# State-space blocks with rows by token, built by two vector passes and four shifted scalar-engine copies

## The chip, the cores and the metric

The kernel runs on one core of one Trainium2 chip. The core has a matrix engine (PE in the profile, TensorE), a vector engine (DVE), a scalar engine (ACT), a general engine (POOL, GpSimd) and a queue that issues the transfers (SP). Each takes its own instructions in order and waits for the others by semaphores. The metric is the time of one execution on the device in microseconds. The kernel before took 2307.09 us (median of three runs, 2300.07 to 2309.19).

## The reference, cut to what matters

The program is two transformer-like blocks on 1024 tokens of width 1024. The change lies in the state-space branch of the first block. It has 32 groups of 16 channels, each with 64 complex states:

```python
def s5_branch(u, ...):
    ug = uf.reshape(bsz, seqlen, 32, 16)
    x_re, x_im = k * (B @ ug)             # complex, 64 states a group
    # h[t] = a * h[t-1] + x[t], complex, by an associative scan over the tokens
    y = einsum('gcp,lbgp->blgc', c_re, h_re) - einsum('gcp,lbgp->blgc', c_im, h_im)
    y = y + d_skip * uf
    y = gelu(y)
    y = y * sigmoid(y @ w_glu + b_glu)
```

The rest (layer norm, latent attention, output projections; a second block with dilated and neighbourhood attention and a gated convolution) is not touched.

## The kernel before, in words

Nothing is written here in the order in which it runs. The program is written by layers, and a scheduler with a timeline of its own then sets the order of every engine's instructions (`schedule_with_timeline_sim=True` where the program is built). So a change of a few instructions also moves others.

In the first block, `block1` projects the normalised tokens with `w_in`. Each of 15 column tiles is two accumulations of 24 matmuls of 512 columns (three products of split operands for each of eight input tiles, lines 135 to 137). The weights of a tile are loaded into `wst`, then ACT rounds them to `wh` (line 102) and POOL computes the rest `wl` (line 111). The first four column tiles are the input u of the state-space branch, which ACT copies out and SP stores to `u_d` with the 8 tokens of a block side by side. Between the later column tiles stand eight calls of `ssm_unit`, one for four groups each. So PE has the dense tiles to do while the units run through the other engines.

A unit treats 8 tokens as one block, so 1024 tokens are 128 blocks. For each of its four groups it needs a 128 x 128 matrix TM from 8 x 16 inputs of a block to its 8 x 16 outputs (block-lower-triangular, and the same along each diagonal), a matrix EM from inputs to states and CS from states to outputs:

- ES (DVE and POOL) is transposed by PE to `sps` and copied by ACT to EM (line 653 and after); KR and CS give `kps`, the effect of an input on an output 0 to 7 tokens later (line 658). DVE adds the skip term `dd` to lag 0.
- DVE builds TM from `kps` in eight passes. Row p of TM is an input (channel c, token s of the block, p = 8c + s), and its columns have to be shifted by s. So pass s multiplies `kps` by a column of the table `cst` that is one where p % 8 = s and adds it s tokens further on: one tensor_scalar of 512 elements and seven scalar_tensor_tensor (lines 90 and 86) of 448, 384, ..., 64 elements, each on all 128 partitions.
- Rotations R (DVE and POOL), the decay RH (POOL, with a zero at the start of each group), the products px = EM U (line 690), the rotated inputs xr, a scan on DVE (line 700), rotation back to h.
- py = TM U + CS h (lines 711 and 712), gelu on ACT, and the store of y by SP.

U is read from `u_d` by one transfer a unit. EM, CS, TM, R and U have two buffers, the others one.

Of the kernel before, what the change touches and what calls it, by code (L numbers as in the profile page):

```python
# [10 lines left out]
F32 = mybir.dt.float32  # L11
F32R = mybir.dt.float32r
I32 = mybir.dt.int32
ALU = mybir.AluOpType
AF = mybir.ActivationFunctionType
# [21 lines left out]

CST = {}
_o = 0
for _n, _w in (("inv_freq", 1), ("sgn", 1), ("shift", 8), ("chan", 16)):  # L40
    CST[_n] = (_o, _w)
    _o += _w
NCST = _o
# [4 lines left out]
def ap_of(t, offset, dims):  # L48
    return bass.AP(tensor=t.tensor, offset=t.offset + offset, ap=dims)


class Kernel:
# [394 lines left out]
    def ssm_open(self):  # L447
        self.sp2, self.spps = self.open("ssmb"), self.open("ssmps", space=PSUM)

    def exp_small(self, x, n, pool, name):  # L450

        nc = self.nc
        a = pool.tile([128, n], F32, name=name + "a")
        r = pool.tile([128, n], F32, name=name + "r")
        p = pool.tile([128, n], F32, name=name + "p")
        e = pool.tile([128, n], I32, name=name + "e")
        self.ts(r, x, -150.0, 89.0, ALU.max, ALU.min)
        M = 12582912.0
        self.ts(a, r, 1.0 / math.log(2.0), M, ALU.mult, ALU.add)
        self.ts(a, a, M, None, ALU.subtract)  # L460
        hi = 0.693359375
        lo = math.log(2.0) - hi
        self.stt(r, a, -hi, r, ALU.mult, ALU.add)
        self.stt(r, a, -lo, r, ALU.mult, ALU.add)
        c = [1.0 / math.factorial(i) for i in range(8)]
        self.ts(p, r, c[7], None, ALU.mult)
        for i in range(6, 0, -1):
            self.stt(p, p, c[i], r, ALU.add, ALU.mult)
        self.ts(p, p, 1.0, None, ALU.add)
        self.ts(a, a, -127.0, 128.0, ALU.max, ALU.min)  # L470
        self.ts(e, a, 127.0, 8388608.0, ALU.add, ALU.mult)
        self.tt(p, p, e.bitcast(F32), ALU.mult)
        return p
# [35 lines left out]
    def ssm_tables(self):  # L509
        nc, I, keep = self.nc, self.I, self.sp  # L510
        p = self.st_
        T = lambda name, shape, dt=F32: p.tile(shape, dt, name=name)
        K = lambda name, shape, dt=F32: keep.tile(shape, dt, name=name)
# [5 lines left out]
        nc.sync.dma_start(self.Cs, I["ssm_bc"][:, 2])  # L519
        self.C2 = K("C2", [128, 32, 16])  # L520
        nc.sync.dma_start(self.C2, I["ssm_bc"][:, 3])
        self.dsk = K("dsk", [128, 32])
        nc.sync.dma_start(self.dsk, I["ssm_d"])
        pos = T("pos", [128, 256], I32)
        for q in range(4):
            nc.sync.dma_start(pos[32 * q:32 * q + 32, :],
# [1 line left out]
        sgn = self.cst[:, CST["sgn"][0]:CST["sgn"][0] + 1]  # L528
# [22 lines left out]
        w = K("pw", [128, 2, 9, 32])  # L551
# [6 lines left out]
        for m in (1, 2, 4):  # L558
            br = wr[:, m:m + 1, :].to_broadcast([128, m, 32])
            bi = wi[:, m:m + 1, :].to_broadcast([128, m, 32])  # L560
            a, b = slice(1, m + 1), slice(m + 1, 2 * m + 1)
# [62 lines left out]
    def ssm_unit(self, u):  # L624

        nc, p, pp = self.nc, self.sp2, self.spps
        b, q = divmod(u, 2)
        G = slice(4 * u, 4 * u + 4)
        T = lambda name, shape, bufs=1, tag=None: p.tile(shape, F32, name=name, tag=tag or name, bufs=bufs)
        f = lambda t: t.rearrange("p a b -> p (a b)")  # L630

        U = T("U", [128, 4, 128], 2)
        nc.sync.dma_start(U, ap_of(self.u_d[b], 64 * q * 1024, [[128, 128], [16 * 1024, 4], [1, 128]]))

        ES = T("ES", [128, 4, 16, 8])
        CS = T("CS", [128, 4, 16, 8], 2)
        tm = T("tm", [128, 4, 16, 8])
        for out, pw, a, c, op in ((ES, self.pv, self.kB1, self.kB2, ALU.add),
                                  (CS, self.pw, self.Cs, self.C2, ALU.subtract)):

            o, t = (y.rearrange("p g c e -> p g e c") for y in (out, tm))
            sh = [128, 4, 8, 16]
            w = lambda i: pw[:, i, 0:8, G].rearrange("p e g -> p g e")[:, :, :, None].to_broadcast(sh)
            x = lambda y: y[:, G][:, :, None, :].to_broadcast(sh)
            self.tt(o, x(a), w(0), ALU.mult, eng=nc.gpsimd)
            self.tt(t, x(c), w(1), ALU.mult)
            self.tt(out, out, tm, op)
        KR = T("KR", [128, 4, 16, 8])
        self.act(KR, self.kB1[:, G][:, :, :, None].to_broadcast([128, 4, 16, 8]), AF.Copy)
        EM = T("EM", [128, 4, 128], 2)  # L650
        ps = pp.tile([128, 4, 128], F32, name="sps", tag="sa", bufs=2)
        for g in range(4):
            nc.tensor.transpose(ps[:, g, :], f(ES[:, g]), self.ident)
        self.act(EM, ps, AF.Copy)

        ps = pp.tile([128, 4, 16, 8], F32, name="kps", tag="sa", bufs=2)
        for g in range(4):
            nc.tensor.matmul(ps[:, g], f(KR[:, g]), f(CS[:, g]), start=True, stop=True)
        o = CST["chan"][0]
        dd = T("dd", [128, 4, 16])  # L660
        self.tt(dd, self.dsk[:, G][:, :, None].to_broadcast([128, 4, 16]),
                self.cst[:, None, o:o + 16].to_broadcast([128, 4, 16]), ALU.mult)
        self.tt(ps[:, :, :, 0], ps[:, :, :, 0], dd, ALU.add)
        TM = T("TM", [128, 4, 16, 8], 2)
        o = CST["shift"][0]
        self.ts(TM, ps, self.cst[:, o:o + 1], None, ALU.mult)
        for s in range(1, 8):
            self.stt(TM[:, :, :, s:], ps[:, :, :, :8 - s], self.cst[:, o + s:o + s + 1], TM[:, :, :, s:], ALU.mult,
                     ALU.add)

        R = T("R", [128, 2, 4, 128], 2)
        rc, rs = R[:, 0], R[:, 1]
        sh = [128, 4, 8, 16]
        v = lambda t: t.rearrange("p g (a b) -> p g a b", a=8)
        A = lambda i: self.RA[:, i, G][:, :, :, None].to_broadcast(sh)
        B = lambda i: self.RB[:, i, G][:, :, None, :].to_broadcast(sh)
        t1 = T("rt", [128, 4, 128])
        self.tt(v(rc), A(0), B(0), ALU.mult, eng=nc.gpsimd)
        self.tt(v(t1), A(1), B(1), ALU.mult)
        self.tt(rc, rc, t1, ALU.subtract)  # L680
        t1 = T("rt", [128, 4, 128])
        self.tt(v(rs), A(1), B(0), ALU.mult, eng=nc.gpsimd)
        self.tt(v(t1), A(0), B(1), ALU.mult)
        self.tt(rs, rs, t1, ALU.add)
        RH = T("RH", [128, 4, 128])
        self.ts(RH, self.rho[:, G][:, :, None].to_broadcast([128, 4, 128]), 1.0, None, ALU.mult, eng=nc.gpsimd)
        nc.gpsimd.memset(RH[:, :, 0:1], 0.0)
        px = pp.tile([128, 4, 128], F32, name="px", tag="sx", bufs=1)
        for g in range(4):
            nc.tensor.matmul(px[:, g, :], EM[:, g, :], U[:, g, :], start=True, stop=True)  # L690
        x2 = T("x2", [128, 4, 128])
        self.act(x2[0:64], px[64:128], AF.Copy)
        self.act(x2[64:128], px[0:64], AF.Copy)
        xr = T("xr", [128, 4, 128])

        self.tt(xr, px, rc, ALU.mult)
        self.tt(x2, x2, rs, ALU.mult)
        self.tt(xr, xr, x2, ALU.subtract)
        gg = T("gg", [128, 4, 128])
        nc.vector.tensor_tensor_scan(f(gg), f(RH), f(xr), 0.0, op0=ALU.mult, op1=ALU.add)  # L700
        g2 = T("g2", [128, 4, 128], 1, "x2")
        self.act(g2[0:64], gg[64:128], AF.Copy)
        self.act(g2[64:128], gg[0:64], AF.Copy)
        h = T("h", [128, 4, 128])
        nc.vector.memset(h[:, :, 0:1], 0.0)
        self.tt(gg, gg, rc, ALU.mult)
        self.tt(g2, g2, rs, ALU.mult)
        self.tt(h[:, :, 1:], gg[:, :, :127], g2[:, :, :127], ALU.add)
        py = pp.tile([128, 4, 128], F32, name="py", tag="sy", bufs=1)
        for g in range(4):  # L710
            nc.tensor.matmul(py[:, g, :], f(TM[:, g]), U[:, g, :], start=True, stop=False)
            nc.tensor.matmul(py[:, g, :], f(CS[:, g]), h[:, g, :], start=False, stop=True)
        y = T("y", [128, 4, 128], 2)
        self.act(y, py, AF.Gelu_apprx_tanh)
        nc.sync.dma_start(ap_of(self.y_d[b], 64 * q * 1024, [[128, 128], [16 * 1024, 4], [1, 128]]), y)
# [1322 lines left out]
def _constants():  # L2038
# [16 lines left out]
    inv = (np.float32(1.0) / np.power(10000.0, e).astype(np.float32)).astype(np.float32)  # L2055
    cst[:, CST["inv_freq"][0]] = np.tile(inv, 4)
    cst[:, CST["sgn"][0]] = np.where(k < 64, -1.0, 1.0)
    o, w = CST["shift"]
    cst[:, o:o + w] = k[:, None] % 8 == np.arange(8)[None]
    o, w = CST["chan"]  # L2060
    cst[:, o:o + w] = k[:, None] // 8 == np.arange(16)[None]

    oh = np.zeros((34, L1W + L2W), np.float32)
    d1 = np.arange(L1W) - 191
# [21 lines left out]
def _layout(v):  # L2086
# [15 lines left out]
    br, bi = f["b_re"][0].transpose(1, 0, 2), f["b_im"][0].transpose(1, 0, 2)  # L2102
    cr, ci = f["c_re"][0].transpose(2, 0, 1), f["c_im"][0].transpose(2, 0, 1)
    r["ssm_bc"] = A(np.stack([np.concatenate(t) for t in ((br, bi), (bi, br), (cr, ci), (ci, cr))], 1))
    r["ssm_d"] = A(np.repeat(f["d_skip"][0].reshape(32, 16).T, 8, axis=0))
    r["w_glu"] = A(_tiles(f["w_glu"][0]))
    wq = f["w_uq"][0].reshape(256, 4, 192)
    wq = np.concatenate([wq[:, :, :128].reshape(256, 512), wq[:, :, 128:160].reshape(256, 128),
# [53 lines left out]
```

## Time and profile before

| | |
|---|---|
| median of three runs | 2307.09 us |
| the profiled execution's own time | 2299.86 us |
| its span | 2298.1 us |
| PE busy over the span | 2116.0 us (92%) |
| DVE busy | 1574.8 us (69%) |
| ACT busy | 983.3 us (43%) |
| POOL busy | 1157.1 us (50%) |
| first instruction of a unit's TM to the last | 121.1 to 308.1 us |

The profile page gives each engine's busy time as a share of the span, then the span in forty slices. The queries on the trace cut out a stretch: which engine is busy for how long in it, which instruction waits for which, and each instruction in order of time. A share over the whole span says nothing of a stage: the units run between about 100 and 320 us, and only their rows tell what limits that stage. A PE that is listed busy counts pipelined matmuls, so what it does not do is seen in its idle time and in the clock that it was granted.

### The profile page before, as it was taken

Reading aid. Unit: us, or ns where it says so; the run is one execution under the profiler, and the core shown is the slowest. Engines: PE = TensorE matmul, PEld = TensorE weight load, DVE = VectorE, ACT = ScalarE, POOL = GpSimd, SP = SyncE. Lnnn points to the kernel's source line nnn. Section 1 sums busy time; section 2 is a strip of 40 time slices with the busy share of each in tenths; the row PEclk is TensorE's granted clock in tenths of the full one; section 3 lists DMA queues with packets and bytes.
Section 4 is the critical chain, followed back from the end, with each engine's and each line's share of the span. In section 5 each row is a group of like instructions: output and inputs, shape, how many; then the busy total and the mean of one; then the engine's idle time right before and its main releaser. Section 6 shows DMA issues by size and latency. Waiting matters only on the chain. (4 is left out here: it accounts for less than half of the span.)

```text
span 2298.1 us, 29156 instructions
## 1 busy us (share of the span) xinstructions
PE 2116.0 (92%) x10144; PEld 1753.3 (76%) x10144; DVE 1574.8 (69%) x2610; ACT 983.3 (43%) x1737; POOL 1157.1 (50%) x742
## 2 busy tenths in 40 slices
PE   6998898899989989999999898995999999999888
PEld 4786777777867778888878786884778888877667
DVE  8969966651587155545766744438877777788997
ACT  4323345432256267656444433224444444454333
POOL 4625547655455455565313425326555555534464
PEclk8998999999999999999999999998999999999998
DMA  7433335555554645655345635441222222232233
GB/s 275 136 93 115 97 121 179 177 160 197 191 179 157 203 128 179 184 167 163 99 142 163 195 116 192 155 137 51 75 90 83 83 83 83 83 137 89 85 115 115
DMA packets 187264, 314.32 MB, mean 137 GB/s; under 512 B 43544, under 2 KB 85100, under 8 KB 187116
## 3 DMA queue, kind: packets, MB, share of 16 engines
q1 hardware_dynamic: 187116, 312.45, 42.3%
q8 instruction: 80, 1.31, 0.2%
q14 instruction: 68, 0.56, 0.1%
HBM read 226.70 MB, written 80.96 MB: 134 GB/s over the span
## 5 line engine op out<-in xcount | busy, mean ns | idle before, releaser
L111 POOL TENSOR_TENSOR wl<-wst,wh 128x1024 fp32r<-128x1024 f32 (+2 forms) x159 | 393.9, 2479 | 500.9 <-ACT wh L102 446.8
L102 ACT ACTIVATE wh<-wst 128x1024 fp32r<-128x1024 f32 (+1 forms) x164 | 168.2, 1028 | 241.5 <-PE ps L136 110.4
L83 POOL TENSOR_TENSOR acc<-acc,wa 128x512 f32<-128x512 f32 x84 | 109.9, 1309 | 14.5 <-ACT wa L102 11.0
L135 PE MATMUL ps<-xh,wh 128*128 128x512 f32 x256 | 103.9, 406 | 4.8 <-DVE kb L83 2.7
L135 PE MATMUL ps<-h0h,wh 128*128 128x512 f32 x256 | 104.3, 407 | 0.7 <-ACT wh L102 0.7
L135 PE MATMUL ps<-h1h,wh 128*128 128x512 f32 x256 | 101.1, 395 | 3.3 <-DVE qz L86 2.1
L137 PE MATMUL ps<-h0h,wl 128*128 128x512 f32 x256 | 103.5, 404 | 0.3 <-POOL wl L111 0.2
L136 PE MATMUL ps<-h0l,wh 128*128 128x512 f32 x256 | 103.3, 403 | 0.0
L136 PE MATMUL ps<-xl,wh 128*128 128x512 f32 x256 | 102.3, 400 | 0.0
L137 PE MATMUL ps<-xh,wl 128*128 128x512 f32 x256 | 102.3, 399 | 0.0
L136 PE MATMUL ps<-h1l,wh 128*128 128x512 f32 x256 | 101.3, 396 | 0.0
L83 POOL TENSOR_TENSOR tb<-rt,grid 128x384 f32<-128x384 f32 x48 | 42.9, 901 | 115.5 <-DVE mx L886 87.8
L137 PE MATMUL ps<-h1h,wl 128*128 128x512 f32 x256 | 100.9, 394 | 0.0
L111 POOL TENSOR_TENSOR wl<-z,wh 128x1024 fp32r<-128x1024 f32 (+1 forms) x38 | 85.8, 2258 | 27.0 <-ACT wh L102 19.9
L1902 PE MATMUL pd<-Ah,wh 128*128 128x512 f32 x224 | 87.2, 403 | 9.5 <-DVE s L83 5.6
L1902 PE MATMUL pd<-Al,wh 128*128 128x512 f32 x224 | 89.1, 399 | 4.4 <-DVE Al L111 4.4
L83 DVE TENSOR_TENSOR z<-r,wst 128x512 f32<-128x512 f32 x40 | 69.4, 1736 | 24.3 <-POOL wl L111 23.5
L1902 PE MATMUL pd<-Ah,wl 128*128 128x512 f32 x224 | 84.1, 395 | 0.8 <-POOL wl L111 0.8
L90 POOL TENSOR_SCALAR wa<-wa,sc 128x512 f32<-128x512 f32 x36 | 57.8, 1605 | 50.4 <-DMA wa<-in_w_ada 43.2
L886 DVE CUSTOM_DVE_ANT_0 sp<-sp,tab 128x256 f32<-128x256 f32 (+1 forms) x128 | 52.8, 424 | 39.1 <-PE sp L163 22.6
L102 ACT ACTIVATE a<-a 128x1024 f32<-128x1024 f32 x22 | 23.4, 1062 | 108.8 <-DVE a L86 108.8
L102 ACT ACTIVATE P<-sp,st 128x256 f32<-128x256 f32 (+1 forms) x128 | 58.9, 463 | 24.2 <-DVE st L886 23.0
(591 smaller groups left out, 7176.5 us busy)
## 6 DMA issues: line engine op xcount, KB each, us to landing
wa<-in_w_ada SPq DMA_DIRECT2D x96, 256.0 KB, 3.5
wst<-in_w_in SPq DMA_DIRECT2D x47, 512.0 KB, 3.8
wst<-in_w_up SPq DMA_DIRECT2D x26, 512.0 KB, 3.3
a_d<-a SPq DMA_DIRECT2D x22, 512.0 KB, 2.6
wst<-in_w_down SPq DMA_DIRECT2D x22, 512.0 KB, 3.6
as<-a_d SPq DMA_DIRECT2D x22, 512.0 KB, 3.5
r<-in_w_up SPq DMA_DIRECT2D x20, 512.0 KB, 3.2
wst<-in_w_out SPq DMA_DIRECT2D x16, 512.0 KB, 3.3
```

What stands on the lines that cost most here:

```text
L83: (eng or self.nc.vector).tensor_tensor(out, a, b, op)
L90: (eng or self.nc.vector).tensor_scalar(out, a, s1, None, op0=op0)
L102: self.nc.scalar.activation(out, a, f, **kw)
L111: self.last_lo = e.tensor_tensor(lo, y, hi.bitcast(F32), ALU.subtract)
L135: first = mm(ps, wh, xh, start=start, stop=False)
L136: mm(ps, wh, xl, start=False, stop=False)
L137: mm(ps, wl, xh, start=False, stop=stop)
L886: self.nc.vector.tensor_tensor_reduce(out=s, in0=s, in1=tab, scale=-1.0, scalar=-NEG, op0=ALU.add, op1=ALU.min, accum_out=m)
L1902: nc.tensor.matmul(ps, w[u][:, 128 * k:128 * k + 128], x[v], start=start and k == i == 0, stop=k == 1 and i == 2, skip_group_check=True)
```

## The change

- The rows of TM are put in the order p = 16s + c (token first). U is loaded to match, by four transfers a unit in place of one. ES and KR get the same order of columns, so both are now written in the order in which they lie. The tables `cst` and `ssm_d` follow.
- TM is now built in three steps. Two DVE passes, over the rows of even and of odd tokens, make Z, which is `kps` unshifted or shifted by one token. Then four copies by ACT, one for each 32 partitions (two tokens), put Z into TM shifted by 0, 2, 4 and 6 tokens. TM has two fixed buffers that POOL zeroes once; the part left of the shift is never written again.
- The skip term `dd` is computed once for all groups in `ssm_tables`, not in each unit.
- The decay RH is spread along the tokens by ACT, not by POOL. POOL still writes the zero.

```diff
-for _n, _w in (("inv_freq", 1), ("sgn", 1), ("shift", 8), ("chan", 16)):
+for _n, _w in (("inv_freq", 1), ("sgn", 1), ("even", 1), ("odd", 1), ("chan", 16)):
...
+        self.TM = [self.sp2.tile([128, 4, 16, 8], F32, name=f"TM{i}") for i in range(2)]
+        for x in self.TM:
+            self.nc.gpsimd.memset(x, 0.0)
...
+        self.dd = K("dd", [128, 32, 16])
+        self.tt(self.dd, dsk[:, :, None].to_broadcast([128, 32, 16]),
+                self.cst[:, None, o:o + 16].to_broadcast([128, 32, 16]), ALU.mult)
...
         U = T("U", [128, 4, 128], 2)
-        nc.sync.dma_start(U, ap_of(self.u_d[b], 64 * q * 1024, [[128, 128], [16 * 1024, 4], [1, 128]]))
-
-        ES = T("ES", [128, 4, 16, 8])
+        for g in range(4):
+            nc.sync.dma_start(U[:, g], ap_of(self.u_d[b], (64 * q + 16 * g) * 1024, [[128, 8], [1024, 16], [1, 128]]))
+
+        ES = T("ES", [128, 4, 8, 16])
...
-            o, t = (y.rearrange("p g c e -> p g e c") for y in (out, tm))
+            tm = T("tm", list(out.shape))
+            o, t = (y if out is ES else y.rearrange("p g c e -> p g e c") for y in (out, tm))
...
-        KR = T("KR", [128, 4, 16, 8])
-        self.act(KR, self.kB1[:, G][:, :, :, None].to_broadcast([128, 4, 16, 8]), AF.Copy)
+        KR = T("KR", [128, 4, 8, 16])
+        self.act(KR, self.kB1[:, G][:, :, None, :].to_broadcast([128, 4, 8, 16]), AF.Copy)
...
-        dd = T("dd", [128, 4, 16])
-        self.tt(dd, self.dsk[:, G][:, :, None].to_broadcast([128, 4, 16]),
-                self.cst[:, None, o:o + 16].to_broadcast([128, 4, 16]), ALU.mult)
-        self.tt(ps[:, :, :, 0], ps[:, :, :, 0], dd, ALU.add)
-        TM = T("TM", [128, 4, 16, 8], 2)
-        o = CST["shift"][0]
-        self.ts(TM, ps, self.cst[:, o:o + 1], None, ALU.mult)
-        for s in range(1, 8):
-            self.stt(TM[:, :, :, s:], ps[:, :, :, :8 - s], self.cst[:, o + s:o + s + 1], TM[:, :, :, s:], ALU.mult,
-                     ALU.add)
+        self.tt(ps[:, :, :, 0], ps[:, :, :, 0], self.dd[:, G], ALU.add)
+
+        Z = T("Z", [128, 4, 16, 8])
+        m = [self.cst[:, CST[n][0]:CST[n][0] + 1] for n in ("even", "odd")]
+        self.ts(Z, ps, m[0], None, ALU.mult)
+        self.stt(Z[:, :, :, 1:], ps[:, :, :, :7], m[1], Z[:, :, :, 1:], ALU.mult, ALU.add)
+        TM = self.TM[u % 2]
+        for k in range(4):
+            r = slice(32 * k, 32 * k + 32)
+            self.act(TM[r, :, :, 2 * k:], Z[r, :, :, :8 - 2 * k], AF.Copy)
...
-        self.ts(RH, self.rho[:, G][:, :, None].to_broadcast([128, 4, 128]), 1.0, None, ALU.mult, eng=nc.gpsimd)
+        self.act(RH, self.rho[:, G][:, :, None].to_broadcast([128, 4, 128]), AF.Copy)
```

How the order moves is shown at two places; the lines of the kernel after stand some ten further down. The first is DVE from the skip term of the seventh unit on (`kps<-kps,dd`; the rows between belong partly to the unit before it, such as h, and to the gates, gt). Before:

```order
L83 TENSOR_TENSOR kps<-kps,dd 128x64
L83 TENSOR_TENSOR h<-gg,g_2243 128x4x127
L90 TENSOR_SCALAR TM<-kps,cst 128x512
L83 TENSOR_TENSOR dd<-dsk,cst 128x64
L86 SCALAR_TENSOR_TENSOR TM<-kps,cst,TM 128x64x7
L83 TENSOR_TENSOR R<-R,rt 128x512
L86 SCALAR_TENSOR_TENSOR TM<-kps,cst,TM 128x64x6
L83 TENSOR_TENSOR xr<-px,R 128x512
L83 TENSOR_TENSOR x_2381<-x_2381,R 128x512
L83 TENSOR_TENSOR rt<-RA,RB 128x512
L86 SCALAR_TENSOR_TENSOR TM<-kps,cst,TM 128x64x5
```

DVE from the same instruction on, after the change:

```order
L83 TENSOR_TENSOR kps<-kps,dd 128x64
L86 SCALAR_TENSOR_TENSOR gt<-gt,ps 128x512
L83 TENSOR_TENSOR rt<-RA,RB 128x512
L90 TENSOR_SCALAR Z<-kps,cst 128x512
L83 TENSOR_TENSOR ES<-ES,tm 128x512
L83 TENSOR_TENSOR R<-R,rt 128x512
L86 SCALAR_TENSOR_TENSOR Z<-kps,cst,Z 128x64x7
L83 TENSOR_TENSOR tm<-C_607,pw 128x4x8x16
L714 MEMSET h 128x4
L83 TENSOR_TENSOR CS<-CS,tm 128x512
L83 TENSOR_TENSOR xr<-px,R 128x512
L83 TENSOR_TENSOR x_2387<-x_2387,R 128x512
```

Before, the passes over TM run on between the products of the input (xr, x) and beyond them; after, both passes over Z stand ahead of these, and four rows of work lie between the second of them and the product that reads x.

The second place is ACT in the same unit, from the gates' row ahead of its EM on. Before:

```order
L102 ACTIVATE gt<-ps 128x512
L102 ACTIVATE EM<-sps 128x512
L102 ACTIVATE g_2243<-gg 64x512 x2
L102 ACTIVATE KR<-kB_814 128x512
L102 ACTIVATE x_2381<-px 64x512 x2
```

ACT after the change:

```order
L102 ACTIVATE gt<-ps 128x512
L102 ACTIVATE EM<-sps 128x512
L102 ACTIVATE KR<-kB_816 128x512
L102 ACTIVATE TM_1105<-Z 32x512
L102 ACTIVATE TM_1105<-Z 32x64x6
L102 ACTIVATE TM_1105<-Z 32x64x4
L102 ACTIVATE TM_1105<-Z 32x64x2
L102 ACTIVATE y<-py 128x512
L102 ACTIVATE x_2387<-px 64x512 x2
L102 ACTIVATE gt<-ps 128x512
L102 ACTIVATE g_2396<-gg 64x512 x2
L102 ACTIVATE RH<-rho 128x512
```

The four copies into TM, and the gelu of the unit before (y), stand ahead of the two copies of px that give x, and RH follows the two copies g of the scan's result.

## Rows read from the trace of the kernel before

**Rows 1.** The page: span, and busy time and share of each engine.

```profile
span 2298.1 us, 29156 instructions
...
PE 2116.0 (92%) x10144; PEld 1753.3 (76%) x10144; DVE 1574.8 (69%) x2610; ACT 983.3 (43%) x1737; POOL 1157.1 (50%) x742
```

**Rows 2.** Busy time by stretch: length, PE, PEld, DVE, ACT, POOL, clock, DMA, GB/s.

```profile
120.00:160.00 40.00, 40.00 (x214) 33.92 (x214) 21.55 (x37) 12.60 (x22) 11.48 (x10) 1.00 0.44 128
160.00:300.00 140.00, 121.91 (x613) 101.82 (x612) 135.15 (x185) 44.21 (x69) 68.68 (x45) 0.94 0.33 95
180.00:200.00 20.00, 13.44 (x54) 10.97 (x55) 19.91 (x25) 5.02 (x7) 10.63 (x6) 0.74 0.34 106
...
300.00:320.00 20.00, 20.00 (x102) 17.03 (x102) 10.43 (x19) 4.53 (x8) 2.78 (x1) 0.99 0.28 87
```

**Rows 3.** What PE waited for from 160 to 300 us: us, times, longest.

```profile
PE py L712 <- DVE h L83: 5.9, 4, 2.0
PE px L690 <- DVE xr L83: 3.7, 1, 3.7
...
PE py L711 <- DVE TM L86: 2.3, 1, 2.3
```

**Rows 4.** DVE by operation, 160 to 300 us: count, busy us, mean ns, idle before.

```profile
L86 DVE SCALAR_TENSOR_TENSOR TM<-kps,cst,TM 128x448 f32<-128x448 f32 (+6 forms) x42 | 20.1, 484 | 0.2
L83 DVE TENSOR_TENSOR h<-gg,g 128x508 f32<-128x508 f32 x6 | 11.1, 1857 | 0.0
...
L83 DVE TENSOR_TENSOR tm<-C,pw 128x512 f32<-128x512 f32 x6 | 7.6, 1265 | 0.0
L83 DVE TENSOR_TENSOR tm<-kB,pv 128x512 f32<-128x512 f32 x5 | 6.6, 1317 | 0.0
...
L83 DVE TENSOR_TENSOR dd<-dsk,cst 128x64 f32<-128x64 f32 x6 | 2.1, 358 | 0.0
```

**Rows 5.** DVE in order of time, 261 to 294 us: start, us, instruction.

```profile
261.10 0.21 DVE L83 TENSOR_TENSOR kps<-kps,dd 128x64 f32<-128x64 f32 x1
...
281.37 0.22 DVE L83 TENSOR_TENSOR kps<-kps,dd 128x64 f32<-128x64 f32 x1
...
283.09 0.67 DVE L86 SCALAR_TENSOR_TENSOR TM<-kps,cst,TM 128x448 f32<-128x448 f32 x1
283.69 0.96 DVE L83 TENSOR_TENSOR R<-R,rt 128x512 f32<-128x512 f32 x1
...
292.18 0.69 DVE L83 TENSOR_TENSOR gg<-gg,R 128x512 f32<-128x512 f32 x1
...
293.64 2.59 DVE L83 TENSOR_TENSOR h<-gg,g 128x508 f32<-128x508 f32 x1
```

**Rows 6.** POOL in order of time, 281 to 294 us.

```profile
281.52 2.58 POOL L83 TENSOR_TENSOR R<-RA,RB 128x512 f32<-128x512 f32 x2 [1.19 <-DVE g L83]
...
290.94 1.77 POOL L90 TENSOR_SCALAR RH<-rho 128x512 f32<-128x512 f32 x1 [5.23 <-DVE gg L700]
...
293.31 2.38 POOL L111 TENSOR_TENSOR wl<-wst,wh 128x1024 fp32r<-128x1024 f32 x1 [0.43 <-ACT wh L102]
```

**Rows 7.** POOL by operation, 160 to 300 us.

```profile
L90 POOL TENSOR_SCALAR RH<-rho 128x512 f32<-128x512 f32 x6 | 9.8, 1636 | 33.8 <-DVE gg L700 33.8
```

**Rows 8.** ACT by shape, 100 to 320 us.

```profile
L102 ACT ACTIVATE x<-px 64x512 f32<-64x512 f32 x16 | 9.5, 593 | 28.7 <-PE px L690 12.2 <-DVE h L83 11.3 <-issue 4.9
...
L102 ACT ACTIVATE wh<-wst 128x256 fp32r<-128x256 f32 x2 | 0.8, 417 | 4.7 <-issue 4.7
...
L102 ACT ACTIVATE li<-lps 8x383 f32<-8x383 f32 x1 | 0.5, 463 | 0.0
```

**Rows 9.** SP's issue of transfers in order of time, 105 to 290 us.

```profile
111.03 0.29 SPq L953 DMA_DIRECT2D oh<-in_oh  x1
...
283.87 0.37 SPq L633 DMA_DIRECT2D U<-u_d  x1
```

**Rows 10.** PE in order of time, 109 to 116 us.

```profile
114.91 1.01 PE L955 MATMUL lps<-oh,rel 34*8 34x511 f32 x2 [2.54 <-DMA oh<-in_oh]
```

More of the change, by code (lines that the diff above doesn't have):

```diff
@@ L521, in ssm_tables @@
         nc.sync.dma_start(self.C2, I["ssm_bc"][:, 3])
-        self.dsk = K("dsk", [128, 32])
-        nc.sync.dma_start(self.dsk, I["ssm_d"])
+        dsk = T("dsk", [128, 32])
+        nc.sync.dma_start(dsk, I["ssm_d"])
+        o = CST["chan"][0]
+        self.dd = K("dd", [128, 32, 16])
+        self.tt(self.dd, dsk[:, :, None].to_broadcast([128, 32, 16]),
+                self.cst[:, None, o:o + 16].to_broadcast([128, 32, 16]), ALU.mult)
         pos = T("pos", [128, 256], I32)
@@ L632, in ssm_unit @@
         U = T("U", [128, 4, 128], 2)
-        nc.sync.dma_start(U, ap_of(self.u_d[b], 64 * q * 1024, [[128, 128], [16 * 1024, 4], [1, 128]]))
-        ES = T("ES", [128, 4, 16, 8])
+        for g in range(4):
+            nc.sync.dma_start(U[:, g], ap_of(self.u_d[b], (64 * q + 16 * g) * 1024, [[128, 8], [1024, 16], [1, 128]]))
+        ES = T("ES", [128, 4, 8, 16])
         CS = T("CS", [128, 4, 16, 8], 2)
-        tm = T("tm", [128, 4, 16, 8])
         for out, pw, a, c, op in ((ES, self.pv, self.kB1, self.kB2, ALU.add),
                                   (CS, self.pw, self.Cs, self.C2, ALU.subtract)):
-            o, t = (y.rearrange("p g c e -> p g e c") for y in (out, tm))
+            tm = T("tm", list(out.shape))
+            o, t = (y if out is ES else y.rearrange("p g c e -> p g e c") for y in (out, tm))
             sh = [128, 4, 8, 16]
@@ L658, in ssm_unit @@
             nc.tensor.matmul(ps[:, g], f(KR[:, g]), f(CS[:, g]), start=True, stop=True)
-        o = CST["chan"][0]
-        dd = T("dd", [128, 4, 16])
-        self.tt(dd, self.dsk[:, G][:, :, None].to_broadcast([128, 4, 16]),
-                self.cst[:, None, o:o + 16].to_broadcast([128, 4, 16]), ALU.mult)
-        self.tt(ps[:, :, :, 0], ps[:, :, :, 0], dd, ALU.add)
-        TM = T("TM", [128, 4, 16, 8], 2)
-        o = CST["shift"][0]
-        self.ts(TM, ps, self.cst[:, o:o + 1], None, ALU.mult)
-        for s in range(1, 8):
-            self.stt(TM[:, :, :, s:], ps[:, :, :, :8 - s], self.cst[:, o + s:o + s + 1], TM[:, :, :, s:], ALU.mult,
-                     ALU.add)
+        self.tt(ps[:, :, :, 0], ps[:, :, :, 0], self.dd[:, G], ALU.add)
[7 more added lines that the diff above has]
+            self.act(TM[r, :, :, 2 * k:], Z[r, :, :, :8 - 2 * k], AF.Copy)
         R = T("R", [128, 2, 4, 128], 2)
@@ L2057, in _constants @@
     cst[:, CST["sgn"][0]] = np.where(k < 64, -1.0, 1.0)
-    o, w = CST["shift"]
-    cst[:, o:o + w] = k[:, None] % 8 == np.arange(8)[None]
+    cst[:, CST["even"][0]] = k // 16 % 2 == 0
+    cst[:, CST["odd"][0]] = k // 16 % 2 == 1
     o, w = CST["chan"]
-    cst[:, o:o + w] = k[:, None] // 8 == np.arange(16)[None]
+    cst[:, o:o + w] = k[:, None] % 16 == np.arange(16)[None]
     oh = np.zeros((34, L1W + L2W), np.float32)
@@ L2104, in _layout @@
     r["ssm_bc"] = A(np.stack([np.concatenate(t) for t in ((br, bi), (bi, br), (cr, ci), (ci, cr))], 1))
-    r["ssm_d"] = A(np.repeat(f["d_skip"][0].reshape(32, 16).T, 8, axis=0))
+    r["ssm_d"] = A(np.tile(f["d_skip"][0].reshape(32, 16).T, (8, 1)))
     r["w_glu"] = A(_tiles(f["w_glu"][0]))
```

## The prediction

> **What bounds the kernel now.** I read the page first. PE is busy 92% of a span of 2298.1 us [rows 1], so a saving elsewhere counts only where PE waits for it. Next I cut the stage of the state-space units into stretches [rows 2]. From 120 to 160 us PE is busy throughout, and again from 300 to 320 us: there nothing that DVE saves can show. Between, from 160 to 300 us, PE is busy for 121.91 of 140 us, and DVE for 135.15. DVE is the engine without a pause, and PE loses time in two ways. [...] A clock of 0.94 over 140 us is worth at most 0.06 x 140 = 8.4 us. PE's whole slack is thus 18 to 26.5 us.
>
> Third, PE's waits in that stretch [rows 3]: for h, for xr, and for TM itself, all results of DVE in a unit. DVE's own time there by operation [rows 4] shows what it does; its order in time beside POOL's [rows 5, 6] shows why one shape takes so different times. A unit begins every 20.3 us (`kps` at 261.10 and 281.37).
>
> The h of 281 to 296 us is the case to look at: DVE's product h takes 2.59 us at 293.64, while POOL's wl runs from 293.31 for 2.38 us, and gg of the same size takes 0.69 us at 292.18. A DVE instruction with both inputs in SBUF is held up by such a POOL instruction. The scalar_tensor_tensor of TM at 283.09, with `kps` in PSUM, takes 0.67 us although POOL's R runs beside it (281.52 to 284.10). So TM's passes are work that POOL does not disturb, and this counts against the change.
>
> **The change part by part.** All sums are for 160 to 300 us, in which six units build their TM (42 scalar_tensor_tensor, seven a unit).
>
> Six of the seven go. The 42 are busy for 20.1 us, the six that stay (the 448-element form, 0.67 us) for 4.0, so 16.1 us of busy time go. Neighbours overlap: the pass at 283.09 lasts 0.67 us and the next begins after 0.60. With 0.08 us for each of 36, DVE gains 16.1 - 2.9 = 13.2 us. The tensor_scalar stays as the first pass over Z, in the same size from PSUM.
>
> The six `dd` go as well: 2.1 us busy, less overlap 1.6 us. The one big `dd` at the beginning is 512 elements with two SBUF inputs: 0.69 us as gg, or 2.6 us as h if POOL reads beside it. DVE has little pause there; I take 0.7 us, lost.
>
> For ES the product tm is now written in order. Its mean is 1317 ns strided [rows 4], the size in order is 690 ns undisturbed [rows 5], and locks are in the first number. Over five instructions the gain lies between 0 and 3.1 us; I take 2.0. The tm for CS (1265 ns) stays strided.
>
> Given back to POOL: POOL is busy 68.68 us of the 140 [rows 2], RH 9.8 of it [rows 7], so it reads two inputs for 58.9 us, 0.42 of the time. Of the 13.2 us that fall away, 0.42 or 5.5 us were passed beside such reading at no cost. Now that reading meets other DVE work. What it costs there has two ends in the rows: R's two instructions, 2.58 us long, cost the DVE instruction at 283.69 only 0.96 - 0.69 = 0.27 us; wl's 2.38 us cost h 1.90. Together 0.44 of POOL's time, so 2.4 us; with some worse alignment I take 3 (from 0 to 13.2, all of the removed time).
>
> RH moves from POOL to ACT, six times 1.64 us [rows 7]. While POOL wrote RH at 290.94 for 1.77 us, gg of DVE took 0.69 us inside it [rows 5, 6], the undisturbed time. So I take nothing for DVE from this. [...]
>
> ACT gets four copies a unit, on 32 partitions, of 512, 384, 256 and 128 elements. The nearest rows [rows 8] are 593 ns for 512, 463 for 383 and 417 for 256 elements, so with an estimate of 0.3 for the last 1.8 us a unit, and about 0.6 for RH. That is 6 x 2.4 = 14 us on an engine busy for 44.21 of 140 us [rows 2], which hides it. What it can cost is delay: ACT copies px to x behind these four. After the second pass over Z, ACT needs 1.8 us, then 0.6 for y and 1.2 for both x copies, 3.6 us. DVE has the tm for CS, CS, xr and a memset in that time, 1.27 + 0.7 + 0.7 = 2.7 us undisturbed. A pause of 0 to 0.9 us a unit results; I take 0.2, or 1 us in all (0 to 5).
>
> U comes in four transfers: 0.37 us of SP each [rows 9], 1.1 us more a unit, on a queue that mostly waits. I cost it at nothing; what covers it is U's second buffer, by which a unit's U can be loaded while the unit before it runs (20 us). POOL's two zeroings of TM, each at most as long as RH (1.64 us for 512 elements), lie before the first unit: nothing.
>
> Before 120 us, PE waits 2.54 us for the load of a table [rows 10] that SP issues only at 111.03 us [rows 9]. POOL, whose freed weight buffers SP needs first, is 1.64 us earlier without RH of the first unit: 0 to 2.5, I take 1.
>
> The sum: -13.2 - 1.6 - 2.0 + 3 + 1 for the stretch is -12.8; +0.7 for `dd` and -1 for the table leave -13.1 us. It stays under PE's slack, so DVE still sets the pace and PE still waits, only less: the unit's period falls to about 18 us. The profiled execution took 2299.86 us, so it would take 2286.8. It lies 7.2 us under the median of the three runs; 2307.09 - 13.1 gives 2294.
>
> **The rivals.** First, *POOL takes it all*. [...] For it speaks that h, R and x are held up already: h has a mean of 1857 ns in [rows 4] where 690 would do. Against it, that POOL reads only 0.42 of the time and cannot fill more. It gives -1.6 - 2.0 + 1 and the ends before 120 us, -3: 2304.
>
> Second, *PE becomes the bound*. If RH too had held DVE up, at 0.44 of its 9.8 us, 4.3 us more fall away; with no pause for x and no give-back to POOL the stretch gains 13.2 + 1.6 + 3.1 + 4.3 = 22 us, inside PE's slack of 18 to 26.5 us. [...]
>
> Third, *ACT's order becomes the bound*, and the kernel slower. In ACT's queue the copies into TM wait for DVE's Z, y waits for PE, and x, g, RH and the next weights wh stand behind both. If PE reaches py late, ACT holds x back, DVE stops, and PE with it. To lose 0.5% it must undo the gain of 13 and cost 11.5 more, 24.5 us or 3.5 us in each of seven units, as long as the whole run of copies, y and x. I give it 3 to 4 us a unit: 2294 + 24.5 = 2319. Against it: most of the time ACT waits for DVE and PE already, and is busy for a third of the stretch.
>
> **How the numbers follow.** About 0.5%, 11.5 us, can be told from no change. The forecast (chance 0.54) has 8 to 18 us around it, 2289 to 2299; some two thirds of its chance lies under 2295.6, the bound of faster. The first rival has 0.25, the second 0.13, the third 0.08. Faster is 0.37 + 0.13 and some of the spread between the first two cases, 0.54; slower 0.07; no change 0.39. The range takes in the second rival with full slack used (2307 - 26.5 = 2280.6) and the first: 2280 to 2307, and leaves out the third and a tail on the fast side.
>
> **What would show it.** In the profile after: two passes over Z a unit of 0.74 and 0.67 us and no others; four ACT copies of 0.3 to 0.6 us; units beginning every 17.5 to 19 us where they began every 20.3; PE's idle time in the stage falling from 18 to 5 to 10 us with a granted clock nearer 1; DVE still without a pause. If h, R and gg grow in the mean, the first rival is at work; if DVE shows pauses that end with ACT's x, the third. PE idle below 3 us would be the second. A change of more than 5 us after 330 us would mean that the shifted order of the attention stage counts, which I have taken as nothing because PE is the bound there.

## The result and the profile after

The kernel after takes 2323.92 us (median of six runs, 2318.07 to 2326.95), the kernel before 2303.68 us in the same comparison. The ratio is 1.0091 (95% interval 1.0072 to 1.0110): it is slower by about 20 us where I had forecast 13 us less.

First the page (span, then busy time of each engine) and the stretches of the units' stage (length, PE, PEld, DVE, ACT, POOL, granted clock, DMA, GB/s), which answer to [rows 1, 2]:

```profile
span 2322.9 us, 29169 instructions
...
PE 2144.7 (92%) x10144; PEld 1765.9 (76%) x10144; DVE 1549.5 (67%) x2555; ACT 1003.9 (43%) x1777; POOL 1149.9 (50%) x736
```

```profile
120.00:160.00 40.00, 40.00 (x195) 33.41 (x194) 18.17 (x28) 13.38 (x23) 7.03 (x7) 0.95 0.46 132
160.00:300.00 140.00, 123.88 (x619) 102.23 (x619) 115.42 (x141) 57.81 (x98) 59.73 (x40) 0.94 0.31 91
180.00:200.00 20.00, 14.72 (x72) 12.14 (x71) 19.89 (x26) 6.40 (x11) 9.12 (x6) 0.83 0.35 107
300.00:320.00 20.00, 19.93 (x106) 16.58 (x105) 10.60 (x17) 8.73 (x16) 5.37 (x2) 1.00 0.30 98
```

DVE lost 19.7 us of work between 160 and 300 us (135.15 before), and PE gained almost nothing: it is still idle for 16.1 us (18.1), at the same clock. PE does about the same number of matmuls (619 for 613). So the relief came and was not passed on. Setting each PE instruction of the two traces side by side tells where the time went. Here and below, "late" is the start in one trace less the start of the same instruction in the trace of before. After is 3.7 us late at 120 us, about level between 200 and 240 (1.3 us early at 220), 7.4 us late at 280, 4 us late at 300 to 320 and 22.6 us late at 520. It then falls back to 16 us by 1400 and rises again from 17 to 28 us between 1480 and 2040. There are three questions: why the units gain nothing, what happens between 320 and 530 us, and why PE drifts in a stage that the change doesn't touch.

**The units.** These groups show what PE and ACT waited for from 160 to 300 us (total, times, longest), in place of [rows 3]:

```profile
PE py L720 <- ACT TM L102: 7.7, 3, 2.9
PE px L699 <- DMA U<-u_d: 3.6, 1, 3.6
PE py L720 <- ACT y L102: 2.6, 1, 2.6
```

```profile
ACT TM L102 <- DVE Z L86: 30.0, 6, 8.8
ACT wh L102 <- DMA wst<-in_w_in: 23.8, 5, 7.6
ACT g L102 <- DVE gg L709: 12.0, 5, 3.6
```

PE hardly waits for DVE's h any more (0.5 us) and no longer for xr, but for ACT. ACT stands for 30 us at its first copy into TM. DVE, which hardly paused before, now has pauses that end with ACT, those before xr among them, the sign that the prediction gave for its third rival:

```profile
DVE gu L86 <- ACT gt L102: 6.0, 1, 6.0
DVE xr L83 <- ACT x L102: 6.0, 4, 2.0
DVE gg L83 <- ACT g L102: 5.6, 4, 1.4
```

One unit in order of time, ACT and then DVE:

```profile
261.41 0.63 ACT L102 ACTIVATE KR<-kB 128x512 f32<-128x512 f32 x1
262.92 0.60 ACT L102 ACTIVATE y<-py 128x512 f32<-128x512 f32 x1 [0.88 <-PE py L721]
270.59 1.93 ACT L102 ACTIVATE TM<-Z 32x512 f32<-32x512 f32 x4 [7.07 <-DVE Z L86]
272.54 1.20 ACT L102 ACTIVATE x<-px 64x512 f32<-64x512 f32 x2
```

```profile
266.15 1.68 DVE L83 TENSOR_TENSOR R<-R,rt 128x512 f32<-128x512 f32 x1
267.75 0.74 DVE L90 TENSOR_SCALAR Z<-kps,cst 128x512 f32<-128x512 f32 x1
268.41 0.95 DVE L83 TENSOR_TENSOR ES<-ES,tm 128x512 f32<-128x512 f32 x1
269.28 0.68 DVE L83 TENSOR_TENSOR rt<-RA,RB 128x512 f32<-128x512 f32 x1
269.88 0.67 DVE L86 SCALAR_TENSOR_TENSOR Z<-kps,cst,Z 128x448 f32<-128x448 f32 x1
...
273.77 0.69 DVE L83 TENSOR_TENSOR xr<-px,R 128x512 f32<-128x512 f32 x1 [0.71 <-ACT x L102]
```

PE ended px at 263.8 us. ACT could have copied it to x then, but its next instruction is the copy into TM, which waits 7.07 us for DVE's second pass over Z. x comes at 272.54, 8.7 us after px, and xr only then. That is the third rival's mechanism, and it is not this unit alone: from the fourth unit to the seventh, x starts 7.3, 8.3, 8.8 and 8.0 us after px is done. The last four units begin (first transpose to `sps`) at 237.2, 257.2, 276.4 and 294.9 us; before they began at 237.7, 251.0, 268.0 and 287.3. By `kps`, from which the prediction took its period of 20.3 us, these four now follow each other after 16.5, 18.4 and 17.5 us, as forecast. But the fourth unit's `kps` comes at 221.9 us where it came at 205.0, and the last one's at the same time as before (300.8 and 300.7): the shorter period only makes up for that delay.

**The attention stage.** Stretches of 40 us, first of before, then of after:

```profile
320.00:360.00 40.00, 34.80 (x210) 29.55 (x210) 29.74 (x82) 25.10 (x58) 33.43 (x30) 1.00 0.52 160
400.00:440.00 40.00, 34.27 (x205) 29.82 (x206) 25.88 (x66) 17.46 (x39) 25.95 (x23) 1.00 0.58 184
440.00:480.00 40.00, 35.99 (x224) 31.47 (x223) 29.94 (x75) 21.65 (x49) 30.69 (x27) 0.96 0.54 159
```

```profile
320.00:360.00 40.00, 35.45 (x186) 29.77 (x184) 27.36 (x67) 23.63 (x52) 29.68 (x28) 0.91 0.50 151
400.00:440.00 40.00, 34.69 (x190) 29.78 (x188) 25.23 (x65) 17.21 (x42) 23.35 (x19) 0.91 0.48 148
440.00:480.00 40.00, 30.09 (x177) 25.72 (x178) 21.13 (x50) 18.17 (x37) 26.21 (x22) 0.91 0.56 167
```

PE is busy about as long in the first two, but for fewer matmuls: the granted clock is 0.91 in place of 1.00. In slices of 2 us it is 0.50 from 340 to 344 us in after and 1.00 from 330 to 338. Summed over 320 to 550 us in slices of 10 us (length times one minus the clock), before lost 1.7 us to the clock and after 15.3. Its pauses are longer too: 4.3 us in front of a projection that waits for `ql`, 3.0 us for `vl`.

**The drift.** PE is busy without a pause from 1700 to 1800 us in both kernels, at a granted clock of 1.00 and in the same order, yet it starts 443 matmuls before and 433 after:

```profile
1700.00:1800.00 100.00, 100.00 (x443) 82.81 (x442) 75.95 (x68) 44.31 (x52) 57.37 (x28) 1.00 0.24 86
```

```profile
1700.00:1800.00 100.00, 100.00 (x433) 81.01 (x432) 75.33 (x67) 45.02 (x52) 55.68 (x27) 1.00 0.24 86
```

By start times the distance between neighbours of 512 columns has two values, 226.7 and 233.3 ns, and which it is goes with the tile that is streamed. t1 to t4, mh, ml, xh, xl, b22, half of od and on, and most of Ah, Al went from the first to the second; uh and ul went the other way. In the built programs these tiles had moved (and a few others with fewer matmuls, such as yg, whose distances are mixed in both kernels): `cst` went from 26 to 20 columns, its allocation in a partition shrank by 32 bytes, and every tile behind it begins 32 bytes lower (t1h at 20192 before, at 20160 after).

### The profile page after: what moved, and what is told of

Its sections match the earlier page's. It is cut to its first block, busy times and chain, and to the rows that moved or that the text cites. A ratio compares the mean times of both kernels' runs of the same rounds, so it can differ in the third digit from the quotient of the medians.

```text
span 2322.9 us, 29169 instructions
## 1 busy us (share of the span) xinstructions
PE 2144.7 (92%) x10144; PEld 1765.9 (76%) x10144; DVE 1549.5 (67%) x2555; ACT 1003.9 (43%) x1777; POOL 1149.9 (50%) x736
```

## The experiments

The theory was threefold: order on ACT, order of the attention stage, and addresses. Twelve kernels were run, four at a time. Their ratios are to the kernel before, measured beside them (2305.48 us for E1 to E4, 2303.64 for E5 to E8, 2304.49 for E9 to E12). In those that hold an order, a table in front of the class moves the lines (102 is 171, 720 is 799).

**E1, the kernel after with the old addresses.**

```diff
-("even", 1), ("odd", 1), ("chan", 16)):
+("even", 1), ("odd", 1), ("chan", 16), ("pad", 6)):
```

> The kernel after, with six unused columns added to the table cst, so that every tile that comes behind it in SBUF lies where it lay before the change; the instructions and their order stay the same. In the two traces the matmuls of 512 columns start 226.7 ns apart where the moving tile begins at an address that is 32 modulo 64, and 233.3 ns where it is 0. By the address theory some 3,180 matmuls go back to 226.7 and 380 to 233.3, net 2,800 x 6.6 ns = 18 us, of which some 4 lie in a stage where PE waits anyway: 2306 to 2310 us against 2324 for the kernel after, and the drift from 1480 us to the end, +10 us, is gone. Rival 'the clock': the wider distance is a matter of the granted clock or of the order, and the padding changes nothing: 2321 to 2327 us.

2318.41 us, ratio 1.0055 (1.0042 to 1.0069), so 5.5 us less than after (8 by the two ratios), not 14 to 18. Instructions and order are those of after. The drift was gone: this trace falls from 9 us behind that of after at 1400 us to 3 us ahead at the end, 12 us, which is some 1,850 matmuls (t, b22, mh, ml, od, on) of 6.6 ns. My count was too large: the 700 of the last stage and those of xh wait for other things. Before 1400 us this profiled run, the slowest of its six, lost up to 9 us to that of after, of which uh and ul explain 2.5. The matmuls, in order of time, after and padded:

```profile
1700.23 0.40 PE L1715 MATMUL u<-t4h,wl 128*128 128x512 f32 x1
1700.46 0.40 PE L1715 MATMUL u<-t4h,wh 128*128 128x512 f32 x1
1700.70 0.40 PE L1715 MATMUL u<-t4l,wh 128*128 128x512 f32 x1
1700.93 0.40 PE L1715 MATMUL u<-t4h,wl 128*128 128x512 f32 x1
```

```profile
1700.16 0.39 PE L1715 MATMUL u<-t4h,wl 128*128 128x512 f32 x1
1700.38 0.39 PE L1715 MATMUL u<-t4h,wh 128*128 128x512 f32 x1
1700.61 0.39 PE L1715 MATMUL u<-t4l,wh 128*128 128x512 f32 x1
1700.84 0.39 PE L1715 MATMUL u<-t4h,wl 128*128 128x512 f32 x1
```

The same instructions stand 0.70 us and 0.68 us apart over three.

**E2, the kernel before with the new addresses** (`("pad", 14)` behind its `chan`).

> The kernel before, with 14 unused columns added to cst, so that every later tile moves by 32 bytes modulo 64, as in the kernel after; instructions and order stay the same. Address theory: th, tl, mh, ml, xh, xl, Ah and Al go from 226.7 to 233.3 ns, uh and ul the other way, and the kernel takes 14 to 18 us more, 2318 to 2322 us, without any of the change. Rival 'the clock': no change, 2301 to 2307 us.

2315.15 us, 1.0045 (1.0030 to 1.0060): 10 us lost with no part of the change. Its PE is 1.4 us late at 1300 us and 13.5 us at 2040.

```profile
1700.00:1800.00 100.00, 100.00 (x433) 80.80 (x432) 76.77 (x69) 45.27 (x53) 53.84 (x26) 1.00 0.22 79
```

**E3, RH on ACT alone** (in before, the diff's last pair of lines).

> The kernel before with one edit of the change alone: RH is spread by ACT. The addresses stay; the scheduler moves few rows among the units, but the order of PE in the attention stage (330 to 520 us) becomes the one of the kernel after. Theory 'order': the loss of 18 us in that stage comes from this order, so the kernel takes 10 to 18 us more than before, 2314 to 2322 us. Rival 'address': the loss there comes from the tiles of that stage (qh, kh, vh, P), which moved by 32 bytes; then this kernel takes 2300 to 2308 us, and the padded kernel after gains in that stage as well and comes to about 2296 us.

2308.28 us, 1.0011 (0.9997 to 1.0025): between the two expectations. The trace shows both signs. PE is 5.0 us early at 300 to 320 us, which RH on ACT gained, and 6.8 us late at 500, with 12.0 us lost to the clock from 320 to 550. The order costs some 12 us there and the gain hides part of it. The attention order is close to that of after but not the same (in the built programs 35 of the stage's 1,412 PE instructions stand elsewhere), and some rows moved among the units, so this run is a weaker test of the order than E5 and E8.

**E4, the copies into TM written behind x.**

```diff
-        for k in range(4): self.act(TM[r, ...], Z[r, ...], AF.Copy)
...
         self.act(x2[64:128], px[0:64], AF.Copy)
+        for k in range(4): self.act(TM[r, ...], Z[r, ...], AF.Copy)
```

> The padded kernel after, with the four copies into TM written behind the two copies px to x, so that ACT takes x first. In the kernel after ACT stands at the first copy into TM for 33.6 us in all between 120 and 300 us, waiting for the second pass over Z, while px is done and x waits behind it (8.7 us in the unit of 262 us). Theory 'ACT's order': without that the units' period falls from 19.5 us to 16 to 18 and the stage to 320 us is 8 to 15 us shorter than in the padded kernel after. Rival 'DVE and its locks': the period stays at 19 to 20 us, since DVE is then the last for the same units; within 4 us of the padded kernel at 320 us. The scheduler also moves rows in later stages, so the verdict is read from the stage of the units.

2315.26 us, 1.0038 (1.0025 to 1.0052). PE is 4 to 5 us earlier than in E1 at 300 to 320 us, but 2.5 us of that are there at 120. It did not test the theory: the scheduler still put one copy ahead of x.

```profile
267.52 0.63 ACT L102 ACTIVATE TM<-Z 32x512 f32<-32x512 f32 x1 [7.04 <-DVE Z L86]
268.16 1.19 ACT L102 ACTIVATE x<-px 64x512 f32<-64x512 f32 x2
```

**E5, E1 with the attention order of before.** For each engine, the names of the 2,233 instructions behind the units, in the order of before:

```diff
+            for e, o in ORDER.items():
...
+                        tc.add_manual_dep(b, last, mybir.DependencyInfo(
+                            mybir.DependencyClass.NoSync, mybir.DependencyReason.DATA), reason="order")
```

> The padded kernel after, with every engine held to the order of the kernel before for the instructions that come behind the units in the program (the attention stage, to about 560 us); the units keep the order of the kernel after. Between 320 and 550 us the granted clock below 1 sums to 15.3 us in the padded kernel after (each 10 us times one minus the clock), to 12.0 with RH on ACT alone, which gives the same order of PE there, and to 1.7 in the kernel before. Theory 'order': the sum falls to 2 to 6 us and the time by 10 to 14 us, from 2318 to 2304-2308. Rival 'late arrival': the stage loses because the units end late and its transfers meet it differently; then the order changes little, 2314 to 2321.

2307.69 us, 1.0016 (1.0003 to 1.0028): 10.7 us under E1 (9 by the ratios), as the theory 'order' has it. The time lost to the clock falls to 3.4 us.

**E6, E5 with x strictly first.**

```diff
+        xc = self.act(x2[64:128], px[0:64], AF.Copy)
+        for k in range(4):
+            r = slice(32 * k, 32 * k + 32)
+            self.after(xc, self.act(TM[r, :, :, 2 * k:], Z[r, :, :, :8 - 2 * k], AF.Copy))
```

> As the kernel with the order of the attention stage, and ACT is held to take both copies px to x before the first copy into TM (in the run with TM written behind x the scheduler still put one copy into TM, waiting 7.0 us for Z, ahead of x). Theory 'ACT's order': x comes 7 to 9 us earlier in a unit, the period of the units falls from 19-20 us to 16-18, and the kernel takes 8 to 12 us less than the one with the attention order alone, 2294 to 2299 us. Rival 'DVE and the locks': DVE is late anyway with the passes and R in front of xr, the period stays at 19 to 20 and the time within 3 us of that kernel.

2292.27 us, 0.9943 (0.9927 to 0.9959): 15.4 us less than E5, more than expected. Stretch, ACT's waits and one unit:

```profile
160.00:300.00 140.00, 130.13 (x689) 110.06 (x689) 123.18 (x156) 65.21 (x111) 67.33 (x42) 0.99 0.35 102
```

```profile
ACT TM L171 <- DVE Z L155: 8.4, 3, 4.8
```

```profile
273.62 0.60 ACT L171 ACTIVATE y<-py 128x512 f32<-128x512 f32 x1 [1.86 <-PE py L800]
274.34 1.20 ACT L171 ACTIVATE x<-px 64x512 f32<-64x512 f32 x2
278.00 1.94 ACT L171 ACTIVATE TM<-Z 32x512 f32<-32x512 f32 x4 [2.46 <-DVE Z L155]
```

x stands right behind y now. Units begin at 233.9, 247.1, 262.1 and 278.9 us, 13 to 17 us apart. PE's idle time is 9.9 us and its clock 0.99, so the gain is twofold. PE is 11.3 us early at 300 to 320 us, against 4.1 us late in E5. In the fifth to seventh unit x starts 0.1 us after px is done, in E5 8.2 to 8.8 us after it. But E6 is not a change of ACT alone. Among the units the scheduler is free, and it gave the other engines a new order there too (about a quarter of DVE's instructions of the units stand elsewhere than in E5), and ACT's waits for weights (wh for `wst`), 23.0 us in E5, fall to 2.8. By `kps` the last four units follow each other after 15.4, 18.3 and 17.0 us, little less than in E5 (16.5, 18.4 and 17.4); the larger difference is that the fourth unit's `kps` comes at 201.5 us, in E5 at 220.5. No run holds the order of the units fixed, so how much of the 15.4 us is ACT's queue and how much the rest of the new order is not separated.

**E7, E5 with the four copies on DVE** (`nc.vector.tensor_copy`).

> As the kernel with the order of the attention stage, with the four copies into TM on DVE in place of ACT: about 2 us more of DVE a unit, and no copy in ACT's queue ahead of x. Theory 'ACT's order': x is free, the period of the units is 17 to 18.5 us and the time 4 to 9 us under the one with the attention order alone, 2297 to 2303 us. Rival 'DVE and the locks': DVE bears 2 us a unit more and the time is 0 to 8 us over it.

2311.58 us, 1.0029 (1.0015 to 1.0042): 4 us over E5, a time in the rival's range. ACT is free for x (it starts 0.1 to 0.2 us after px in the last four units), but DVE is near its old load:

```profile
160.00:300.00 140.00, 120.69 (x617) 101.09 (x616) 131.32 (x174) 48.76 (x77) 61.17 (x41) 0.94 0.32 94
```

The 4 us do not arise among the units, though: PE is 3.1 us late at 300 us, in E5 4.1. They come behind them, where this run loses 10.2 us to the clock from 320 to 550 although the order of the stage is held. So among the units neither DVE's relief with TM ahead of x (E5) nor ACT's freedom with DVE's old load (E7) gives a gain; E6 has both and gains. Here too the scheduler moved other rows of the units.

**E8, the kernel before with the attention order of after.**

> The kernel before, unchanged but for the order of the attention stage, in which every engine is held to the order of the kernel after. Theory 'order': granted clock lost between 320 and 550 us rises from 1.7 to 8-15 us, and the time by 5 to 13 us, from 2305 to 2310-2318. Rival 'late arrival': within 3 us of the kernel before.

2321.02 us, 1.0071 (1.0056 to 1.0087): 17 us lost, with the code and the addresses of before. Its PE is 0.5 us late at 300 us and 19.3 at 520, and 11.9 us go to the clock. By itself this order costs nearly as much as the kernel after loses. E5 gets back 10.7, so the two measurements of it lie 6 us apart. No run holds the kernel before to its own order, so what the holding itself costs is not shown; E5, held in the same way, gained.

```profile
440.00:480.00 40.00, 32.76 (x195) 28.38 (x196) 24.33 (x58) 18.38 (x38) 28.29 (x24) 0.91 0.57 171
480.00:520.00 40.00, 33.25 (x183) 28.42 (x182) 20.96 (x50) 13.44 (x30) 24.80 (x21) 0.91 0.55 163
```

**E9, E6 without the padding.**

> The kernel with x strictly first and the attention order of before, but without the padding of cst: every tile lies as in the kernel after, instructions and order are those of the padded one (2292.3 us). Address theory, with the size that the two padded runs show (the matmuls from 1480 to 2040 us alone, 12 us; the 700 of the last stage wait for other things): 10 to 12 us more than with the padding, 2301 to 2305 us. Rival 'the padding acted by something else': 2289 to 2296 us.

2300.71 us, 0.9986 (0.9974 to 0.9998), 8.4 us over E6 (10 by the ratios): a third measurement of the addresses, at or a little under the expected size.

**E10, E6 with v1t eight columns wider, so that uh and ul move.**

> The padded kernel with x strictly first and the attention order of before, and v1t eight columns wider, so that uh and ul too begin at 32 modulo 64. Address theory: the 380 matmuls with uh and ul go from 233.3 to 226.8 ns, 2 to 2.5 us less, 2289 to 2291 us; some tiles of two norms move with them, at nothing. Rival 'the lower part of SBUF or the stage': uh stays at 233 ns and the time at 2290 to 2295 us.

2286.80 us, 0.9929 (0.9911 to 0.9948), the fastest of all, though its interval overlaps that of E6. uh went to 228.1 ns, near the expected 226.8, ul only to 231.0.

**E11, E6 with the scheduler's own attention order.**

> The padded kernel with x strictly first, and the attention stage in the order that the scheduler gives by itself (neither that of before nor that of after). The units are as in the run with the order held, 15 us gained. Theory 'order': what it loses is the granted clock between 320 and 550 us beyond the 3.4 us of the held order, 0 to 12 us: 2292 to 2304 us, and the time follows that sum. Rival 'late arrival': the units end early, so the stage loses nothing, 2290 to 2294 us.

2295.29 us, 0.9954 (0.9939 to 0.9969): not told apart from E6. The trace, with 11.9 us lost to the clock from 320 to 550 us against 3.4 in E6, cannot be set against that median: it is from the slowest of the twelve executions (2301.20 us), and E6's is from the fastest of its six (2286.40). In these two PE falls 9 us further behind between 320 and 520 us, so there the time does follow the sum. The twelve executions differ in the same sense: the three with a mean clock of 0.969 or 0.970 took 2285.5 to 2290.1 us, the other nine (0.963 to 0.967) 2292.8 to 2301.2. How often this order loses the clock, one trace cannot say.

**E12, the kernel before with the weights moved by 32 bytes.**

```diff
+        self.open("sh", "right").tile([128, 8], F32, name="shift32")
         self.wp = self.open("w", "right")
```

> The kernel before with an empty tile of 32 bytes under the weights' buffers: wh and wl now begin at 0 modulo 64 (32 before), and so do the tiles on their side of SBUF (h0, h1, b11, b21, od1, ymh); tiles of the other side (t, m, Ah, xh, od0) stay at 32 and uh, ul at 0. Instructions and order stay. Rule 'the moving tile's own address': t, m and Ah stay at 226.7 ns, uh at 233.3, and b11, b21, od1 and part of h0, h1 rise to 233.3; 5 to 10 us more, 2309 to 2314 us. Rule 'moving tile against weights': t, m and Ah rise to 233.3, uh falls to 226.8, b11 and b21 stay; 12 us more, 2314 to 2318 us.

2315.21 us, 1.0052 (1.0035 to 1.0070). The distances mostly follow the second rule, moving tile against weights (addresses from the built programs, distances from the traces):

| kernel | begin of moving tile / of weights, modulo 64 | distance, ns |
|---|---|---|
| before | t, mh: 32 / 32 | 226.7 to 227.2 |
| before | uh: 0 / 32 | 233.3 |
| after | t, mh: 0 / 32 | 233.3 to 233.6 |
| after | uh: 32 / 32 | 227.4 |
| E12 | t, mh: 32 / 0 | 232.6 to 233.8 |
| E12 | uh: 0 / 0 | 228.9 |

```profile
1700.00:1800.00 100.00, 100.00 (x433) 80.80 (x432) 76.79 (x69) 44.30 (x52) 53.73 (x25) 1.00 0.22 79
```

The tiles t lie where they lay in before, and only the weights moved. E2 moved the other side by 32 bytes, and its mean distances are the same, tile by tile: 233.4 ns for t, 228.9 for uh. In both b11 and b21 stand at 229.3 ns (226.8 in before) with equal remainders, which the second rule does not explain.

## Why the prediction was wrong

The medians add up in order: from after, 2323.9, the old addresses take 5.5 (E1), the old attention order 10.7 (E5), x ahead of TM, with the order of the units that came with it, 15.4 (E6). By the ratios, each to its own kernel before, the three steps are 8, 9 and 17 us. Two of these the prediction had at nothing or at 1 us, and one it did not have.

- *What bounds the kernel.* Right for the stage: PE waited for DVE, and E6, E9 and E10, early by 11.3 to 13.0 us at 320 us, show that the forecast size could be had there.
- *DVE's sum* (-13.2, -1.6, -2.0). Right in sign and about in size. The passes over Z take 0.745 and 0.677 us, the big `dd` 0.63. tm for ES fell only from 1317 to 1130 ns, 0.9 us for 2.0.
- *Given back to POOL* (+3). Of mixed sign: h fell from 1857 to 918 ns, where the first rival had it grow, while R rose from 1020 to 1619 ns over ten, 6 us. DVE's busy time still fell by 19.7 us, so this rival is out. What the prediction calls locks is in the traces a DVE row that lasts longer beside a POOL row: in before tm for ES lasts 2.04 us at 235.31 us, where POOL's product for CS runs from 234.79 for 1.63 us, and 1.07 to 1.20 us in its other four rows from 160 to 300 us. What holds it is not shown.
- *RH at nothing.* E3 is 5 us early before the attention stage, which would suit the second rival. But in the trace of before gg runs beside RH in four units (it starts at 133.24, 227.30, 255.19 and 292.18 us, overlapping RH by 0.3 to 0.5 us and not lying inside it) and takes 0.69 us each time, so no row shows RH holding it up, and no run shows the second rival's 4.3 us. POOL's freed time, 9.8 us [rows 7], and the moved rows are the other candidates; no run separates them.
- *ACT's copies, 1.8 us a unit.* They take 1.93 us. The step that failed in this stage is the next one, "a pause of 0 to 0.9 us a unit results; I take 0.2, or 1 us in all". I counted ACT's work from the second pass over Z and took it that px was not done earlier. But the order printed in the section on the change already had ES and R between the passes, and on ACT all copies stand ahead of x: x waits for the slowest of what is queued in front of it, 7 to 9 us in four units running. The third rival named this and asked for "3.5 us a unit" to make the kernel slower, and I gave it 0.08. Among the units the whole gain went, not more: PE is 3.7 us late at 120 us and 4 at 300. The trace shows ACT's queue as a cause of that; E6, in which this wait is gone, does not separate it from the other rows that moved there.
- *U's four transfers at nothing.* One wait of 3.6 us in after, none among PE's longer waits in E6: small and not separated.
- *The table, -1.* It did not happen: SP issues the load at 113.4 us and PE waits 2.8 us.
- *The attention stage, "taken as nothing because PE is the bound there".* This failed most, and it is what made the kernel slower. PE was busy 90% of 320 to 560 us before and is 88% after, with a mean granted clock of 0.94 in place of 0.99: a PE that is busy for nine tenths of a stage still had pauses to lengthen and a clock to lose. The same instructions in the scheduler's new order cost 17 us in E8, and put back into the old order they gave back 10.7 in E5. The clock lost from 320 to 550 us is 1.7 to 10.2 us in the eight traces with the old order and 11.9 to 18.7 in the six with another. The prediction named the test for it (over 5 us after 330) but no price.
- *Addresses* were in no term. E1, E2 and E9 give 5.5, 10 and 8.4 us (8, 10 and 10 by the ratios).

What stays open: which of the reordered instructions starts the pauses, how E6's gain divides between ACT's queue and the other moved rows, and the 4 us that E5 is behind before (in its trace PE is 3.3 us late at 120 us already, ahead of most of the units' work).

## What to carry to other kernels

Where work moves to an engine with a queue in order, read the new order of that queue and ask what stands behind the first instruction that waits; a short copy can hold back the one on which the loop turns. When a scheduler sets the order, a local edit is an edit of later stages too: hold their order fixed (E5, E8) before judging it, and remember that what is not held moves again with the next edit (E6, E7). A trace shows one execution: before its numbers are set against a median, see where that execution lies among the others (E11). And compare the addresses of the tiles before and after: a constant table that is 24 bytes shorter in each partition cost 5 to 10 us here.

## What the runs showed of the hardware

At a granted clock of 1.00 the matmuls of 512 columns that stream t and mh start 226.7 to 227.2 ns apart in before, where the moving tile and the weights begin at the same address modulo 64. They start 233.3 to 233.6 ns apart in after and 232.6 to 233.8 in E12, where the two differ by 32. uh stands at 233.3 ns in before, where they differ, and at 227.4 in after and 228.9 in E12, where they are equal. E12 moved the weights' side alone, and the matmuls with moving tiles of the other side slowed by some 6.6 ns each; what the two streams share is not shown. Some streams do not follow: ymh and yml stay at 233.3 ns in before, after, E10 and E12 with equal remainders, and b11 and b21 rise from 226.8 to 229.3 in E2 and E12, so this is not a complete rule and its mechanism is not shown.
